# Two hybrid decoder layers on one core: five weight low halves per layer made by an adding DMA

## The chip, the cores and the metric

The kernel runs on 1 core of one Trainium2 chip. The metric is the device time of one execution in microseconds (us). Before the change three runs took 714.25, 714.69 and 716.07 us (median 714.69). The engines named here are PE (TensorE, matrix products), DVE (VectorE), ACT (ScalarE), POOL (GpSimd) and SP (SyncE, which in this kernel starts all the DMA transfers).

## The reference

Two decoder layers work on a residual stream of 256 tokens by 1024 channels, all in float32. Cut to what matters, one layer is:

```python
proj = x @ w_in                      # 1024 -> q_a, k_a, v_a, a, b, z, q_b, k_b, v_b
o_a = gdn_mixer(q_a, k_a, v_a, a, b, z, ...)   # causal conv, chunked delta rule: a 64x64
                                               # triangular system per head and chunk
o_b = moba_mixer(q_b, k_b, v_b, pos)           # partial rotary, softmax attention, 8 heads
mix = concat([o_a, o_b]) @ w_out
x = layer_norm(alpha * x + mix)
hid = causal_dwconv(x @ w_up) + b
gate, val = split(hid)
x = layer_norm(alpha * x + (silu(gate) * val) @ w_down)
```

## The kernel before, in words

All weights come as chunks of 128 partitions by 1024 float32 (512 KB). PE multiplies in a rounded form of float32 (the tile type F32R), so every weight chunk `w` is taken as a rounded high half `h` and a low half `w - h`, and the stream `x` as `xh` and `xl` in the same way. A projection (`proj`) is 24 matmuls: eight pairs `h*xh` and `h*xl`, then eight `lo*xh`. A chunk is loaded by SP into one of six `wr` buffers (`load_raw`, line 181), ACT copies its two halves of 512 columns into a `wh` tile (line 196, which rounds), and DVE (POOL for some chunks of the MLP) subtracts, `wl = wr - wh` (line 197). There are five `wh` and five `wl` buffers, so the splitting runs up to five chunks ahead of PE. A projection writes one of two PSUM buffers `pj`. ACT and DVE must empty it before the next projection but one may begin: for the delta-rule heads ACT makes a first tap (line 424) and DVE three more (line 427), for the attention heads ACT copies (line 447), DVE shuffles and multiplies (lines 449 and 450), and POOL finishes the rotary (lines 455 and 456, the unit `rp`; here called the ropes).

The mixing stage of a layer is written as a list of units, the string `ORDER[l]`: `ka:0` is the projection of head 0 of `k_a`, `qb:3` of pair 3 of `q_b`, `kk`, `decay`, `sk`, `am` build the triangular matrices A (lines 505 and 507 on DVE), `solve` inverts the 16x16 diagonal blocks on POOL (28 dependent instructions, lines 527 and 529) after a way through DRAM (`da`, line 512, `T<-da`, line 518), `ex` brings the inverses back through DRAM (`dx`, line 531, `PT<-dx`, line 538) and spreads them on DVE (line 543), `lt` is the first matmul on them (PE, line 560). Letters behind `@` keep a unit's instructions on that engine behind those of the unit before. Within these bounds a scheduler places the instructions; each engine then works through its own list in order, and an instruction that waits holds up all behind it on that engine.

Three tiles outside the split rings matter: `oh` and `ol` (the two halves of the mixer's output, needed late in a layer; `oh` also takes the raw input at the very start) and `lnb` (the rows of a layer norm, needed at a layer's two norms). In the kernel before `oh` and `ol` are taken at the top of a layer.

Of the kernel before, what the change touches and what calls it, by code (L numbers as in the profile page):

```python
# [11 lines left out]
F32 = mybir.dt.float32  # L12
F32R = mybir.dt.float32r
# [3 lines left out]
AF = mybir.ActivationFunctionType  # L17
OP = mybir.AluOpType
# [51 lines left out]


ORDER = ("""
ab ka:0@A ab2@G ka:2@P qb:0@GP ka:3@G ka:1 kk:0 decay@AGD kk:1@PG kb:0@G kb:2@G sk@GP ld:0@P ld:1@DG kb:3@G am:0@A
vb:1@DAGP qb:1@GP kb:1@G rp@DG am:1@AG qb:2@G qb:3 va:2@GP va:0@G va:3 rk@G solve@G va:1@D qa:1 qa:0@P ex@DPA lt@GP s:0@DA lx@DAP
tr:0@AD mt:32:0@GAP mx:32:0@G mt:32:1@G vt:0@G rp@GP mx:32:1@PAG pv:0 mt:64:0@GDPA mt:64:1@AG s:1@AGD
qa:3@G qa:2@GP mx:64:0@PG tr:1@PA mx:64:1@D z:0 s:2@GADP pv:1@GA sq:0@DG vt:1@ADP zsol:0@D az tr:2@A s:3@GDP pv:2@AG
tr:3@PGD zsol:1@A z:2@G qk@GP sq:1@GDA o:0@ADP z:1@G wu:1@PGA pv:3@AGP o:1@GDP w:0:5 w:0:4@D w:1:4@PDA z:3@PD w:1:6@G
w:0:7@GD w:1:5@GPD ot:1@AP ot:0@G wu:0@PA w:0:6@A
""", """
vb:1@APDG ab@GD ka:0@G ab2@G ka:3 qb:0@P ka:2@G ka:1@P kk:0 decay@ADG kb:0 kk:1@GA kb:2 sk@AP kb:3@G kb:1@PG qb:2  # L80
rp@GPD qb:3@GP am:0@PA qb:1@DP am:1@AG ld:0@GP va:1@P va:0@GP rk@AG va:2@G ld:1@D solve@GP va:3@P qa:1 ex@D lt@DAP s:0@GD
lx@DAPG mt:32:0@A mt:32:1@AG vt:0@PD rp@GAD tr:0@AP qa:0 mx:32:0 pv:0@A mx:32:1@AD mt:64:0@AGD mt:64:1@DGP s:1@A
qa:3 qa:2@P mx:64:1@APD tr:1@P z:0@G s:2@G sq:0@D vt:1@DG mx:64:0@GDP pv:1 zsol:0@DGP az@A tr:2@DA s:3@GD pv:2@AG
# [6 lines left out]
def hybrid_kernel(ctx, tc, xT, x, wab, wch, par, lnrow, cst, msk, out):  # L90
    nc = tc.nc
    pe, act, dve, pool, sp = nc.tensor, nc.scalar, nc.vector, nc.gpsimd, nc.sync
# [5 lines left out]
    res = ctx.enter_context(tc.tile_pool(name="res", bufs=1))  # L98
# [104 lines left out]
    def load_chunk(l, ci, hp=None, le=None):  # L203
        return split(load_raw(l, ci), hp, le)

    def proj(ps, l, ci, le=None):
        h, lo = load_chunk(l, ci, le=le)
        h = h.rearrange("p (k m) -> p k m", k=KT)
        lo = lo.rearrange("p (k m) -> p k m", k=KT)
        for k in range(KT):  # L210
            pe.matmul(ps, h[:, k, :], xh[:, k, :], start=k == 0, stop=False)  # L211
            pe.matmul(ps, h[:, k, :], xl[:, k, :], start=False, stop=False)  # L212
        for k in range(KT):
            pe.matmul(ps, lo[:, k, :], xh[:, k, :], start=False, stop=k == KT - 1)  # L214
# [12 lines left out]
    def rsqrt(v, n, eng):  # L227
# [3 lines left out]
        for i in range(2):  # L231
# [106 lines left out]
    vb = vb_first()  # L338
    const_prep()

    for l in range(DEPTH):
# [24 lines left out]
        qb, kb = mt("qb", [128, 4, S]), mt("kb", [128, 4, S])  # L366
# [3 lines left out]
                st[nm] = mt("vz", [128, 2, HG, 128] if nm != "va" else [128, HG, S], 2)  # L370
            return st[nm]

        oh = res.tile([128, KT, S], F32R, name="oh")
        ol = res.tile([128, KT, S], F32R, name="ol")
        G, T, st = [], {}, {}

        def u_ab():
            abr = small.tile([128, KT, 8], F32, name="abr", bufs=1)
# [277 lines left out]
        def u_pv(p):  # L656
            PT0, PT1 = st["PT", p]
            po = ps_m()[:, 0:256]
            for a in range(2):
                rs = slice(64 * a, 64 * a + 64)  # L660
                hs = slice((2 * p + a) * 64, (2 * p + a) * 64 + 64)
                pe.matmul(po[rs, :], vb[:, 0, hs], PT0[:, a, :], start=True, stop=False, skip_group_check=True)  # L662
                pe.matmul(po[rs, 128:256], vb[:, 1, hs], PT1[:, a, :], start=False, stop=True, skip_group_check=True)
            act.activation(oh[:, 4 + p, :], po, AF.Copy)
            dve.tensor_tensor(ol[:, 4 + p, :], po, oh[:, 4 + p, :].bitcast(F32), op=OP.subtract)

        def u_vt(b):
            ps = heads(ps_a())
# [46 lines left out]
        def u_ot(b):  # L715
            bs = slice(b * 128, b * 128 + 128)
            ps = heads(ps_m())
            for h in range(HG):
                pe.transpose(ps[:, h, :], st["on", b][:, h, :], ident)
            of = mt("PT0", [128, HG, 128], 2)  # L720
            dve.scalar_tensor_tensor(of, ps, pr[:, P_NG:P_NG + 1], zs[:, :, bs], op0=OP.mult, op1=OP.mult)
            act.activation(oh[:, 0:4, bs], of, AF.Copy)
            dve.tensor_tensor(ol[:, 0:4, bs], of, oh[:, 0:4, bs].bitcast(F32), op=OP.subtract)

        acc = []

# [14 lines left out]
        def w_out(t, ks, stop=False):  # L741
            ts = slice(t * 128, t * 128 + 128)
            if not acc:
                acc.extend([[ps_a() for _ in range(2)] for _ in range(2)])
            start, done[t] = not done[t], done[t] + list(ks)
            for k in ks:
                if k not in ws:
                    ws[k] = load_chunk(l, C_WO + k)
            down(t, [(oh[:, k, ts], ol[:, k, ts], ws[k]) for k in ks], start, stop)

        def u_wu(i):
            nm = ("qb", "kb", "ka", "qa")[2 * i:2 * i + 2]
# [52 lines left out]
        lnb = load_lnb(l, 0)  # L805
# [64 lines left out]
        lnb = load_lnb(l, 1)  # L870
# [133 lines left out]
```

## Time and profile before

| | |
|---|---|
| median of three runs | 714.69 us |
| the profiled execution | 714.04 us, of which 712.3 us from its first to its last instruction (the span) |
| granted TensorE clock, mean over the span | 0.984 |
| PE busy | 688.6 us (97%), 5056 matmuls |
| DVE busy | 576.9 us (81%) |
| ACT busy | 400.8 us (56%) |
| POOL busy | 197.2 us (28%) |
| DMA | 118.07 MB, mean 166 GB/s |

PE's busy time counts the ends of pipelined matmuls, so a "full" stretch can still hold short gaps; where PE stands still for long, its busy time in a stretch falls below the stretch's length. The clock is given as a share: 1.00 is 2.4 GHz, and a half is 1.2 GHz, the lower of its two levels. Layer 0's mixing stage runs from about 20 to 150 us, layer 1's from about 367 to 500 us; between them lie the MLPs.

### The profile page before, as it was taken

Reading aid. Unit: us, or ns where it says so; the run is one execution under the profiler, and the core shown is the slowest. Engines: PE = TensorE matmul, PEld = TensorE weight load, DVE = VectorE, ACT = ScalarE, POOL = GpSimd, SP = SyncE. Lnnn points to the kernel's source line nnn. Section 1 sums busy time; section 2 is a strip of 40 time slices with the busy share of each in tenths; the row PEclk is TensorE's granted clock in tenths of the full one; section 3 lists DMA queues with packets and bytes.
Section 4 is the critical chain, followed back from the end, with each engine's and each line's share of the span. In section 5 each row is a group of like instructions: output and inputs, shape, how many; then the busy total and the mean of one; then the engine's idle time right before and its main releaser. Section 6 shows DMA issues by size and latency. Waiting matters only on the chain.

```text
span 712.3 us, 13664 instructions
## 1 busy us (share of the span) xinstructions
PE 688.6 (97%) x5056; PEld 618.6 (87%) x5056; DVE 576.9 (81%) x1273; ACT 400.8 (56%) x908; POOL 197.2 (28%) x200
## 2 busy tenths in 40 slices
PE   8989999999999999999999989999999999999994
PEld 5979888787999999999888988888789999999994
DVE  5899877599788887778879987776998888887756
ACT  5644466546666665656355445556476566666531
POOL 0045700013333343332002382000153333333413
PEclk9999999999999999999999997999999999999998
DMA  8876351521766665656153437134246766666201
GB/s 313 305 244 192 78 198 40 199 89 61 276 220 194 211 222 184 202 181 205 60 201 129 144 94 222 61 103 159 66 150 234 233 213 194 214 206 202 70 1 60
DMA packets 41217, 118.07 MB, mean 166 GB/s; under 512 B 10176, under 2 KB 12992, under 8 KB 40640
## 3 DMA queue, kind: packets, MB, share of 16 engines
q1 hardware_dynamic: 41152, 117.21, 49.6%
q8 instruction: 40, 0.66, 0.3%
q14 instruction: 25, 0.20, 0.1%
HBM read 114.84 MB, written 2.36 MB: 165 GB/s over the span
## 4 chain that ended last, share of the span: by engine, by line
PE 86%; DVE 9%; ACT 1%; issue 1%; DMA 1%; SPq 0%; DVEq 0%; ACTq 0%
PE pj L211 16%; PE pj L212 15%; PE pj L214 15%; PE ac L732 8%; PE ac L733 8%; PE ac L734 8%; DVE wl L197 3%; PE pj L225 1%; PE pj L222 1%; DVE cv L427 1%; PE mx L619 1%; PE pj L223 1%; PE mx L313 1%; DMA wr<-in_wch_dram 1%; PE mx L662 1%
## 5 line engine op out<-in xcount | busy, mean ns | idle before, releaser
L196 ACT ACTIVATE wh<-wr 128x512 fp32r<-128x512 f32 x376 | 219.5, 622 | 108.2 <-PE pj L212 49.1
L211 PE MATMUL pj<-xh,wh 128*128 128x256 f32 x1024 | 258.6, 289 | 7.4 <-DVE cv L427 7.4
L212 PE MATMUL pj<-xl,wh 128*128 128x256 f32 x1024 | 257.2, 287 | 0.0
L197 DVE TENSOR_TENSOR wl<-wr,wh 128x512 fp32r<-128x512 f32 x292 | 206.7, 736 | 28.2 <-ACT wh L196 14.7
L211 PEld LDWEIGHTS pj<-xh,wh 128*128 128x128 f32 x1024 | 198.6, 194 | 11.4 <-issue 5.4
L212 PEld LDWEIGHTS pj<-xl,wh 128*128 128x128 f32 x1024 | 199.1, 194 | 1.6
L197 POOL TENSOR_TENSOR wl<-wr,wh 128x512 fp32r<-128x512 f32 x84 | 116.2, 1405 | 204.9 <-ACT wh L196 199.7
L214 PE MATMUL pj<-xh,wl 128*128 128x256 f32 x1024 | 147.6, 286 | 0.0
L214 PEld LDWEIGHTS pj<-xh,wl 128*128 128x128 f32 x1024 | 134.2, 194 | 0.4 <-issue 0.2
L733 PE MATMUL ac<-wh,fal 128*128 128x512 f32 x144 | 56.4, 392 | 0.0
L732 PE MATMUL ac<-wh,fah 128*128 128x512 f32 x144 | 56.1, 392 | 0.0
L734 PE MATMUL ac<-wl,fah 128*128 128x512 f32 x144 | 56.0, 389 | 0.0
L842 DVE TENSOR_TENSOR fal<-fth,fah 128x256 fp32r<-128x256 f32 (+1 forms) x48 | 36.8, 767 | 17.3 <-ACT fah L841 17.0
L828 DVE SCALAR_TENSOR_TENSOR fc<-pj,par,fc 128x255 f32<-128x255 f32 x80 | 38.1, 476 | 4.2 <-ACT fc L824 2.8
L828 DVE SCALAR_TENSOR_TENSOR fc<-pj,hw,fc 128x255 f32<-128x255 f32 x80 | 38.3, 478 | 3.7 <-ACT fc L824 2.4
L817 POOL TENSOR_SCALAR hw<-par 128x66 f32<-128x66 f32 x2 | 2.1, 1048 | 139.2 <-DVE wlh L197 139.2
L839 DVE SCALAR_TENSOR_TENSOR fth<-fth,fc 128x256 f32<-128x256 f32 (+1 forms) x48 | 23.6, 492 | 20.1 <-ACT fth L838 20.1
L841 ACT ACTIVATE fah<-fth 128x256 fp32r<-128x256 f32 (+1 forms) x48 | 18.9, 393 | 34.8 <-DVE fth L840 34.8
L838 ACT ACTIVATE fth<-fc 128x256 f32<-128x256 f32 (+1 forms) x48 | 19.2, 400 | 31.7 <-DVE fc L828 31.5
L427 DVE SCALAR_TENSOR_TENSOR cv<-pj,par,cv 128x255 f32<-128x255 f32 (+2 forms) x72 | 33.8, 472 | 0.6 <-ACT cv L424 0.3
L734 PEld LDWEIGHTS ac<-wl,fah 128*128 128x128 f32 x144 | 27.1, 188 | 5.9
L732 PEld LDWEIGHTS ac<-wh,fah 128*128 128x128 f32 x144 | 27.1, 189 | 4.8
(257 smaller groups left out, 1030.5 us busy)
## 6 DMA issues: line engine op xcount, KB each, us to landing
wr<-in_wch_dram SPq DMA_DIRECT2D x195, 512.0 KB, 4.1
lnb<-in_lnrow_dram SPq DMA_DIRECT2D x4, 1024.0 KB, 4.6
xres<-in_x_dram SPq DMA_DIRECT2D x2, 512.0 KB, 6.8
da<-A SPq DMA_DIRECT2D x4, 256.0 KB, 3.4
ka<-in_wch_dram SPq DMA_DIRECT2D x2, 512.0 KB, 4.5
qa<-in_wch_dram SPq DMA_DIRECT2D x2, 512.0 KB, 5.1
qb<-in_wch_dram SPq DMA_DIRECT2D x2, 512.0 KB, 4.8
kb<-in_wch_dram SPq DMA_DIRECT2D x2, 512.0 KB, 5.7
```

What stands on the lines that cost most here:

```text
L196: ih = act.activation(h[:, s], raw[:, s], AF.Copy)
L197: il = le.tensor_tensor(lo[:, s], raw[:, s], h[:, s].bitcast(F32), op=OP.subtract)
L211: pe.matmul(ps, h[:, k, :], xh[:, k, :], start=k == 0, stop=False)
L212: pe.matmul(ps, h[:, k, :], xl[:, k, :], start=False, stop=False)
L214: pe.matmul(ps, lo[:, k, :], xh[:, k, :], start=False, stop=k == KT - 1)
L427: dve.scalar_tensor_tensor(cv[:, o:], ps[:, :S - o], w[:, j:j + 1], cv[:, o:], op0=OP.mult, op1=OP.add)
L732: pe.matmul(ps, a_h, w_h[:, ns], start=start and i == 0, stop=False, skip_group_check=True)
L733: pe.matmul(ps, a_l, w_h[:, ns], start=False, stop=False, skip_group_check=True)
L734: pe.matmul(ps, a_h, w_l[:, ns], start=False, stop=stop and i == len(items) - 1, skip_group_check=True)
L828: dve.scalar_tensor_tensor(cv[:, d], ps[:, d.start - o:d.stop - o], w[:, q:q + 1], cv[:, d], op0=OP.mult, op1=OP.add)
L839: dve.scalar_tensor_tensor(th, th, 1.0, cg[:, ts], op0=OP.add, op1=OP.mult)
L842: dve.tensor_tensor(al, th, ah.bitcast(F32), op=OP.subtract)
```

## The change

For five chunks of a layer the low half is no longer made by DVE. A unit `p:n`, placed in the order ahead of the projection that uses its chunk, loads the chunk as before; ACT writes the rounded high half into one half of a tile and the same number negated into the other; a DMA that POOL starts then reads the chunk once more from DRAM and adds it onto the negated half, which leaves `w - h` there. The tile is `oh`, `lnb` or `ol`, at a time when the layer does not hold anything else in it; `oh` and `ol` are taken for the mixer's output only at its first write (`mo`). `proj` takes a prepared pair from `pre` where there is one. The chunks are `kb:0`, `kb:2`, `kb:3` in both layers, then `qb:3` and `va:2` in layer 0, `qb:1` and `va:0` in layer 1.

```diff
+PRE = (((C_KB, "oh"), (C_KB + 2, "ol"), (C_KB + 3, "lnb"), (C_QB + 3, "oh"), (C_VA + 2, "ol")),
+       ((C_KB, "oh"), (C_KB + 2, "ol"), (C_KB + 3, "lnb"), (C_QB + 1, "oh"), (C_VA, "ol")))
...
-ab ka:0@A ab2@G ka:2@P qb:0@GP ka:3@G ka:1 kk:0 decay@AGD kk:1@PG kb:0@G kb:2@G sk@GP ld:0@P ld:1@DG kb:3@G am:0@A
+ab ka:0@A p:0 ab2@G ka:2@P p:1 qb:0@GP p:2 ka:3@G ka:1 kk:0 decay@AGD kk:1@PG kb:0@G kb:2@G sk@GP ld:0@P ld:1@DG kb:3@G p:3 am:0@A
...
+    pre = {}
+
+    def sum_split(l, ci, home):
+        raw = load_raw(l, ci)
+        both = res.tile([128, 2, 1024], F32R, name=home)
+        for v, sign in ((0, 1.0), (1, -1.0)):
+            for q in range(0, 1024, 512):
+                i = act.activation(both[:, v, q:q + 512], raw[:, q:q + 512], AF.Copy, scale=sign)
+                if "act" in hold:
+                    tc.add_manual_dep(i.ins, hold["act"].name, nosync, reason="norm first")
+        pool.dma_start(both[:, 1, :], wch[l, ci], accum_op=OP.add)
+        pre[l, ci] = both[:, 0, :], both[:, 1, :]
+
     def proj(ps, l, ci, le=None):
-        h, lo = load_chunk(l, ci, le=le)
+        h, lo = pre.pop((l, ci), None) or load_chunk(l, ci, le=le)
...
-        oh = res.tile([128, KT, S], F32R, name="oh")
-        ol = res.tile([128, KT, S], F32R, name="ol")
         G, T, st = [], {}, {}
+
+        def mo(name):
+            if name not in st:
+                st[name] = res.tile([128, KT, S], F32R, name=name)
+            return st[name]
+
+        def u_p(n):
+            ci, home = PRE[l][n]
+            sum_split(l, ci, home)
```

In the changed kernel line numbers are 2 higher above the new helper (198 is the ACT copy of a split, 199 the subtraction, 215 the new ACT copies, 218 the adding DMA) and 22 higher in the units (477 and 478 are the ropes, 449 the taps).

On POOL, layer 0, from the start of the list to the rotary of `kb:2` (`km` are masks, `gx` belongs to the decay, `sw` to the rotary), there stood before:

```order
L167 CAST km<-wr 128x640
L455 ISA
L455 TENSOR_TENSOR sw<-sw,kt 128x256
L418 TENSOR_TENSOR gx<-kt,g_l 128x512 x2
L456 TENSOR_TENSOR qb<-qb,sw 128x256
L455 TENSOR_TENSOR sw<-sw,kt 128x256
L456 TENSOR_TENSOR kb<-kb,sw 128x256
```

and now:

```order
L218 DMA oh<-in_wch_dram 128x1024
L218 DMA ol<-in_wch_dram 128x1024
L218 DMA lnb<-in_wch_dram 128x1024
L169 CAST km<-wr 128x640
L440 ISA
L440 TENSOR_TENSOR gx<-kt,g_l 128x512 x2
L218 DMA oh<-in_wch_dram 128x1024
L218 DMA ol<-in_wch_dram 128x1024
L477 TENSOR_TENSOR sw<-sw,kt 128x256 x2
L478 TENSOR_TENSOR qb<-qb,sw 128x256
```

Three adding DMAs stand ahead of the masks, two more ahead of all ropes; the last of them (for `va:2`) reuses the tile of `kb:2`, so it waits until PE is through with `kb:2` and ACT has then written four copies.

On ACT, layer 0, around the decay (`E`) and the emptying of `kb:0` and `kb:2`, there stood before:

```order
L465 ACTIVATE E_243<-ac 128x4x128
L465 ACTIVATE E_244<-ac 128x512
L447 ACTIVATE kb<-pj 128x256
L196 ACTIVATE wh<-wr 128x512 x2
L471 ACTIVATE E_243<-ac 128x4x128
```

and now:

```order
L469 ACTIVATE kb<-pj 128x256
L487 ACTIVATE E_243<-ac 128x4x128
L487 ACTIVATE E_244<-ac 128x512
L215 ACTIVATE oh<-wr 128x512 x3
L493 ACTIVATE E_243<-ac 128x4x128
L215 ACTIVATE oh<-wr 128x512
L198 ACTIVATE wh<-wr 128x512 x6
L469 ACTIVATE kb<-pj 128x256
L215 ACTIVATE ol<-wr 128x512 x4
```

Eight new copies stand between the emptyings of PSUM, and six copies of later chunks come ahead of them.

On DVE, layer 0, from the decay's `gx` to the third head of `ka`, there stood before:

```order
L413 CAST g_h<-g 128x8
L197 TENSOR_TENSOR wl<-wr,wh 128x512
L414 TENSOR_TENSOR g_l<-g,g_h 128x8
L418 TENSOR_TENSOR gx<-kt,g_h 128x512 x2
L427 SCALAR_TENSOR_TENSOR cv<-pj,par_216,cv 128x254
L197 TENSOR_TENSOR wl<-wr,wh 128x512
L427 SCALAR_TENSOR_TENSOR cv<-pj,par_216,cv 128x253
L427 SCALAR_TENSOR_TENSOR cv<-pj,par_216,cv 128x255
L197 TENSOR_TENSOR wl<-wr,wh 128x512
L430 SCALAR_TENSOR_TENSOR ka<-th,cv 128x256
```

and now:

```order
L435 CAST g_h<-g 128x8
L472 TENSOR_TENSOR qb<-qb,kt 128x256
L436 TENSOR_TENSOR g_l<-g,g_h 128x8
L440 TENSOR_TENSOR gx<-kt,g_h 128x512 x2
L449 SCALAR_TENSOR_TENSOR cv<-pj,par_216,cv 128x255
L199 TENSOR_TENSOR wl<-wr,wh 128x512
L449 SCALAR_TENSOR_TENSOR cv<-pj,par_216,cv 128x254
L199 TENSOR_TENSOR wl<-wr,wh 128x512
L449 SCALAR_TENSOR_TENSOR cv<-pj,par_216,cv 128x253
L519 SCALAR_TENSOR_TENSOR scr,sk<-ac,kt 128x128
```

The subtractions that stand here now are those of `ka:1`; those of `kb:0`, which stood here before, are gone.

## Rows read from the trace of the kernel before

**Rows 1.** Stretches: length, busy PE, PEld, DVE, ACT, POOL, clock, DMA share, GB/s.

```profile
20.00:30.00 10.00, 10.00 (x84) 9.73 (x83) 9.46 (x26) 8.36 (x19) 0.72 (x1) 1.00 0.79 264
30.00:46.00 16.00, 14.16 (x98) 12.36 (x96) 16.00 (x48) 8.59 (x18) 6.09 (x5) 1.00 0.67 227
46.00:70.00 24.00, 23.97 (x196) 23.57 (x195) 23.80 (x68) 11.19 (x25) 12.06 (x11) 1.00 0.73 240
70.00:76.00 6.00, 3.95 (x20) 3.98 (x21) 4.76 (x10) 1.31 (x4) 4.98 (x14) 0.72 0.36 110
380.00:392.00 12.00, 11.19 (x82) 9.86 (x81) 11.94 (x32) 5.98 (x14) 4.67 (x4) 1.00 0.35 116
...
416.00:424.00 8.00, 5.96 (x38) 5.51 (x36) 6.11 (x14) 3.39 (x7) 6.82 (x16) 0.79 0.13 51
424.00:437.00 13.00, 11.38 (x103) 10.47 (x99) 11.78 (x21) 6.04 (x14) 7.79 (x16) 1.00 0.42 101
437.00:448.00 11.00, 11.00 (x157) 10.34 (x153) 7.55 (x24) 4.97 (x17) 0.00 (x0) 0.53 0.65 240
```

**Rows 2.** The chain of waits, 58 to 76 us: start, duration, engine and line.

```profile
66.32 1.75 DVE wl L197 x3
...
70.99 0.41 DVE cv L427
...
71.42 0.49 DVE cv L427
...
72.05 0.43 PE pj L211
```

**Rows 3.** Groups of DVE, 28 to 72 us: busy us, mean ns.

```profile
L197 DVE TENSOR_TENSOR wl<-wr,wh 128x512 fp32r<-128x512 f32 x29 | 21.2, 745 | 0.0
```

**Rows 4.** Groups of ACT, 20 to 46 us.

```profile
L196 ACT ACTIVATE wh<-wr 128x512 fp32r<-128x512 f32 x22 | 12.3, 623 | 0.0
```

**Rows 5.** The chain of waits, 46 to 60 us.

```profile
48.85 0.96 PE pj L214 x8
```

**Rows 6.** Groups of POOL, 31 to 64.3 us: the ropes ahead of the solve.

```profile
L455 POOL TENSOR_TENSOR sw<-sw,kt 128x256 f32<-128x256 f32 x6 | 5.1, 853 | 15.2 <-DVE sw L449 12.4 <-DVE pl L409 2.8
L456 POOL TENSOR_TENSOR kb<-kb,sw 128x256 f32<-128x256 f32 x4 | 3.5, 877 | 1.7 <-DVE kb L450 1.3 <-DVE rsz L236 0.4
...
L456 POOL TENSOR_TENSOR qb<-qb,sw 128x256 f32<-128x256 f32 x2 | 2.2, 1115 | 0.4 <-DVE qb L450 0.4
```

**Rows 7.** Timeline of POOL, layer 0: the solve's first and last but one step.

```profile
66.06 2.14 POOL L527 TENSOR_TENSOR T<-T,P 64x14 f32<-64x14 f32 x1 [1.88 <-DVE P L524]
...
81.16 0.27 POOL L527 TENSOR_TENSOR T<-T,P 64x14 f32<-64x14 f32 x1
```

**Rows 8.** Timeline of SP's DMA queue, layer 0: the inverses are read back.

```profile
85.32 0.38 SPq L538 DMA_DIRECT2D PT<-dx  x1
```

**Rows 9.** Timeline of DVE, 89 to 93 us: the first inverse is spread.

```profile
90.98 0.42 DVE L543 TENSOR_TENSOR gX<-PT,kt 128x256 f32<-128x256 f32 x1
```

**Rows 10.** Timeline of PE, layer 0: the first matmul on the inverses.

```profile
91.45 0.66 PE L560 MATMUL ac<-gX,A 64*64 64x32 f32 x16
```

**Rows 11.** Timeline of ACT, 396 to 398 us: the emptying of `kb:2`, layer 1.

```profile
397.09 0.37 ACT L447 ACTIVATE kb<-pj 128x256 f32<-128x256 f32 x1
```

**Rows 12.** Timeline of POOL, layer 1: the solve's first step.

```profile
412.82 0.60 POOL L527 TENSOR_TENSOR T<-T,P 64x14 f32<-64x14 f32 x1 [1.07 <-DVE P L524]
```

**Rows 13.** Timeline of SP's DMA queue, layer 1: the inverses are read back.

```profile
432.32 0.38 SPq L538 DMA_DIRECT2D PT<-dx  x1
```

**Rows 14.** Timeline of PE, layer 1: the first matmul on the inverses.

```profile
436.66 0.66 PE L560 MATMUL ac<-gX,A 64*64 64x32 f32 x16
```

**Rows 15.** DMA issues by line: count, KB each, median us to landing.

```profile
wr<-in_wch_dram SPq DMA_DIRECT2D x195, 512.0 KB, 4.1
...
kt<-in_cst_dram SPq DMA_DIRECT2D x1, 522.0 KB, 8.4
...
PT<-dx SPq DMA_DIRECT2D x2, 128.0 KB, 3.3
```

More of the change, by code (lines that the diff above doesn't have):

```diff
@@ L72 @@
 ORDER = ("""
-ab ka:0@A ab2@G ka:2@P qb:0@GP ka:3@G ka:1 kk:0 decay@AGD kk:1@PG kb:0@G kb:2@G sk@GP ld:0@P ld:1@DG kb:3@G am:0@A
-vb:1@DAGP qb:1@GP kb:1@G rp@DG am:1@AG qb:2@G qb:3 va:2@GP va:0@G va:3 rk@G solve@G va:1@D qa:1 qa:0@P ex@DPA lt@GP s:0@DA lx@DAP
+ab ka:0@A p:0 ab2@G ka:2@P p:1 qb:0@GP p:2 ka:3@G ka:1 kk:0 decay@AGD kk:1@PG kb:0@G kb:2@G sk@GP ld:0@P ld:1@DG kb:3@G p:3 am:0@A
+vb:1@DAGP p:4 qb:1@GP kb:1@G rp@DG am:1@AG qb:2@G qb:3 va:2@GP va:0@G va:3 rk@G solve@G va:1@D qa:1 qa:0@P ex@DPA lt@GP s:0@DA lx@DAP
 tr:0@AD mt:32:0@GAP mx:32:0@G mt:32:1@G vt:0@G rp@GP mx:32:1@PAG pv:0 mt:64:0@GDPA mt:64:1@AG s:1@AGD
@@ L79 @@
 """, """
-vb:1@APDG ab@GD ka:0@G ab2@G ka:3 qb:0@P ka:2@G ka:1@P kk:0 decay@ADG kb:0 kk:1@GA kb:2 sk@AP kb:3@G kb:1@PG qb:2
+vb:1@APDG ab@GD ka:0@G p:0 ab2@G ka:3 p:1 qb:0@P p:2 ka:2@G ka:1@P kk:0 decay@ADG kb:0 kk:1@GA kb:2 sk@AP kb:3@G p:3 kb:1@PG p:4 qb:2
 rp@GPD qb:3@GP am:0@PA qb:1@DP am:1@AG ld:0@GP va:1@P va:0@GP rk@AG va:2@G ld:1@D solve@GP va:3@P qa:1 ex@D lt@DAP s:0@GD
@@ L663, in u_pv @@
                 pe.matmul(po[rs, 128:256], vb[:, 1, hs], PT1[:, a, :], start=False, stop=True, skip_group_check=True)
-            act.activation(oh[:, 4 + p, :], po, AF.Copy)
-            dve.tensor_tensor(ol[:, 4 + p, :], po, oh[:, 4 + p, :].bitcast(F32), op=OP.subtract)
+            act.activation(mo("oh")[:, 4 + p, :], po, AF.Copy)
+            dve.tensor_tensor(mo("ol")[:, 4 + p, :], po, mo("oh")[:, 4 + p, :].bitcast(F32), op=OP.subtract)
         def u_vt(b):
@@ L721, in u_ot @@
             dve.scalar_tensor_tensor(of, ps, pr[:, P_NG:P_NG + 1], zs[:, :, bs], op0=OP.mult, op1=OP.mult)
-            act.activation(oh[:, 0:4, bs], of, AF.Copy)
-            dve.tensor_tensor(ol[:, 0:4, bs], of, oh[:, 0:4, bs].bitcast(F32), op=OP.subtract)
+            act.activation(mo("oh")[:, 0:4, bs], of, AF.Copy)
+            dve.tensor_tensor(mo("ol")[:, 0:4, bs], of, mo("oh")[:, 0:4, bs].bitcast(F32), op=OP.subtract)
         acc = []
@@ L748, in w_out @@
                     ws[k] = load_chunk(l, C_WO + k)
-            down(t, [(oh[:, k, ts], ol[:, k, ts], ws[k]) for k in ks], start, stop)
+            down(t, [(mo("oh")[:, k, ts], mo("ol")[:, k, ts], ws[k]) for k in ks], start, stop)
         def u_wu(i):
```

## The prediction

> **What bounds the kernel now.** I read the stretches first. Over most of the program PE is full and the clock stands at 1.00, and there nothing that DVE does less can help. The exceptions that the change can reach lie in the first half of each mixing stage [rows 1]. In layer 0 PE is busy 14.16 of the 16 us from 30 to 46 and 3.95 of the 6 us from 70 to 76, while DVE is busy for all of the former and for 23.80 of the 24 us between. In layer 1 PE lacks 0.81 us from 380 to 392, 2.04 from 416 to 424 and 1.62 from 424 to 437. The reader is to see that DVE is the full engine ahead of each gap. The chain of waits names the instruction: before PE goes on at 72.05 it runs through DVE alone, subtractions of weights (line 197) and the taps that empty PSUM (line 427) in turn [rows 2]. So PE waits for a PSUM buffer, and the buffer's taps wait in DVE's list behind subtractions. The groups give their weight: 29 subtractions, 21.2 us of the 44 us from 28 to 72, 0.745 us each [rows 3].
>
> The gaps cost a second time through the clock. It is 0.72 over 70 to 76 and 0.79 over 416 to 424, right where PE stood still, so part of these stretches ran at the lower level, 1.2 GHz: (1 - 0.72) * 6 = 1.7 us and (1 - 0.79) * 8 = 1.7 us [rows 1]. Recoverable are 1.84 + 2.05 + 1.7 = 5.6 us in layer 0 and 0.81 + 2.04 + 1.62 + 1.7 = 6.2 us in layer 1. The clock of 0.53 from 437 to 448 belongs to a stretch of small matmuls behind a gap; I leave it out of the sum.
>
> A second chain runs beside this one, on POOL: ropes, then the solve, then two transfers through DRAM, then the first matmul on the inverses (line 560). PE meets it at 91.45 and at 436.66 [rows 10, 14]. The read-back starts at 85.32 and 432.32 [rows 8, 13] and lands a median 3.3 us later [rows 15], at 88.6 and 435.6; DVE then needs 0.42 us [rows 9]. So PE arrives only 2.4 us (91.45 - 88.6 - 0.42) and 0.6 us after the inverses could be there. If PE gains more than that, the solve must move too. This is the gate of the whole change.
>
> **The change part by part.** *DVE* loses ten subtractions per layer, 10 * 0.745 = 7.5 us [rows 3]: six (`kb:0`, `kb:2`, `kb:3`) ahead of the matrices A, four behind. The gap at 70 is 2.05 us, so DVE's backlog there goes; what is late next is the gate.
>
> *ACT* gets twenty copies where it had ten, 10 * 0.56 = 5.6 us more per layer (12.3 / 22 = 0.56 back to back [rows 4]). In layer 0 twelve of the twenty come before 32 us, into a stretch where ACT is busy 8.36 of 10 already [rows 1]; six copies more are 3.4 us against the 1.64 us left. Since `ka:2` to `ka:1` are split just ahead of PE there, I count PE 1 us late (bounds 0 and 1.8). From 30 to 70 ACT is busy 19.8 of 40 us, so the other copies hide behind PE's work; without that cover they would cost at most 2.2 us, one group of four. In layer 1 the first copies fall between the norm's steps, where ACT waits; I take 0.
>
> *POOL* gets five DMA starts per layer. No row shows a DMA started by POOL. The nearest are SP's DMA instruction, 0.38 us [rows 8], and POOL's longest step of the solve, 2.14 us [rows 7]; I take 1 us. They matter by their place. The last two stand ahead of all ropes, and the last waits until PE is done with `kb:2` and ACT has written four copies (2.2 us). In layer 0 `kb:2` ended at 48.85 + 0.96 = 49.8 [rows 5]; with 1.84 us of gap gone and 1 us lost to ACT I put it at 48.5 to 49. Then 2.2 + 1 us, so the ropes begin near 52, where before they were spread from 31 on. Their twelve instructions last 5.1 + 3.5 + 2.2 = 10.8 us [rows 6]: POOL is ready for the solve at 62.5. DVE's part (line 524) was what the solve waited for before, 1.88 us [rows 7]; it follows A, which loses six subtractions (4.5 us) ahead of it, so it comes at about the same time. The solve begins near 62.5 instead of 66.06, 3.5 us earlier. In layer 1 `kb:2` was emptied at 397.09 [rows 11]; 1.1 us earlier, plus 2.2 + 1 + 10.8, gives 410.0 against 412.82 [rows 12], 2.8 us earlier.
>
> The Trainium skill (SBUF — State Buffer, section "SBUF: two separate sides") holds a rule against this: descriptors of a DMA started on GpSimd cannot be written while DVE runs in a two-port mode, and it tells of 620 ns that became 3100. No row here shows such a DMA; an estimate by that page would put each start 2.5 us later. It is taken up under the gate rival.
>
> *The adding transfer* has no row either. Below it lies a plain chunk, 4.1 us; above, twice the slowest of that size, 2 * 8.4 = 16.8 us, as it reads DRAM and the tile [rows 15]. I take twice the plain one, 8 us. It has time: PE takes 24 * 0.12 = 2.9 us per chunk (0.96 / 8 a matmul [rows 5]); between `kb:2` and `va:2` lie five chunks, and the low half is wanted 16 matmuls later, 48.7 + 14.4 + 1.9 = 65, against a start at 51. That is 14 us free; in layer 1, with six chunks, 17. The engines' share is 0.73 at most stretches here [rows 1], so ten more transfers fit; plain loads run several chunks ahead.
>
> **The sum.** Layer 0: PE could be at line 560 at 91.45 - 5.6 + 1 = 86.9; the gate opens at 88.6 - 3.5 + 0.42 = 85.5. PE decides: 4.6 us gained. Layer 1: PE could be there at 430.5; the gate opens at 435.6 - 2.8 + 0.42 = 433.2. The gate decides: 3.4 us, and PE waits 2.7 us. Gaps of 2 us have brought 1.7 us of lower clock at 70 and 416, so I take off one such stretch. 4.6 + 3.4 - 1.7 = 6.3 us. The profiled execution took 714.04 us (span 712.3 and 1.7 around it), 0.65 under the median; so 707.7 for it, 708.4 for the median. What follows line 560 is full on PE, so the gain stays.
>
> **The rivals.** *The gate does not move.* POOL starts its ropes late, or a start lasts 4 to 5 us, and the solve begins when it did. Then the gains are 2.4 and 0.6 us, less 1.7 for the clock: 1.3 us, 713.4. For it: POOL's list puts two waiting starts ahead of twelve ropes. Against: POOL waited 1.88 and 1.07 us for DVE before [rows 7, 12]. The page's estimate above would give this time as well.
>
> *The solve shortens too.* The same step takes 2.14 us at 66.06, amid subtractions, and 0.27 at 81.16 [rows 7]. With DVE ahead of its work the first steps may lose 3 us; PE then decides in both layers, 4.6 + 6.2 us, and no new gap lowers the clock: 10.8 us, 703.9; if the stretch of 0.53 goes as well, 702. For that the Trainium skill (SBUF — State Buffer, section "Who interferes with whom") has a rule: a DVE instruction with two SBUF inputs contends with GpSimd's reads. By that rule the time is this rival's; the trace agrees, with 2.14 against 0.27.
>
> *The adding transfer is slow,* which ends on the other side. Past 14 us, PE stands at `va:2` in layer 0, us for us; past 17 at `va:0` in layer 1. At 22 us: layer 0 4.6 - 8 = -3.4, layer 1 gets 3.4 - (5 - 2.7) = 1.1, and long gaps lower the clock in both, -3.4: 5.7 us slower, 720.4. It decides from about 18 us. For it: the transfer reads two sources and shares the engines with loads that took 8.4 us in a crowd. Against: the median of 4.1.
>
> That the change doesn't do what it says I give nothing: the lists of both kernels show the subtractions gone.
>
> **How the numbers follow.** The forecast has 0.58, with its own range 704.5 to 711.5 (ACT's loss 0 to 1.8, the lower clock 0 to 3.4). The gate rival has 0.17, the shorter solve 0.10, the slow transfer 0.15. A difference under 0.3%, 2.1 us, is about what a measurement of this kernel cannot tell from none. So faster is 0.58 + 0.10 = 0.68, the same 0.17, slower 0.15. The range goes from 702.5, nearly all of the shorter solve, to 717, which takes in the gate rival and the nearer half of the slow transfer. The predicted time is 708.5.
>
> **What would show it.** DVE at line 449 without a wait of PE on it near 70 and 416, and fewer than 23 us busy of 24 from 46 to 70: the first step is right. The solve's first step at 62 to 63.5 and 409 to 411: the gate moved; at 66 or later, the gate rival. PE's line 582 (560 before) near 87 and 433. A wait of PE at `va:2` or `va:0` on the DMA into `ol`: the slow transfer. I am wrong if ACT's copies at line 215 hold the emptying of PSUM back by more than 2 us, or if POOL's starts last longer than 4 us.

## The result, and the profile after

The changed kernel takes 724.78 us (median of four runs, 723.15 to 728.11) against 715.38 us for the kernel before on the same chip: the ratio is 1.0134, with a 95% interval from 1.0103 to 1.0165. It is 1.3% slower, where 708.5 us was forecast, and it lies outside the stated range (702.5 to 717). The profiled execution took 726.39 us, with a span of 724.6 us. Executions that came out over 1.5% above the fastest of their kernel, at a lower granted clock, are left out of the medians and ratios below.

The stretches of the changed kernel come first, with the columns of [rows 1] (busy PE, PEld, DVE, ACT, POOL, then clock, DMA share, GB/s).

```profile
20.00:30.00 10.00, 9.78 (x79) 9.25 (x77) 7.83 (x26) 9.87 (x23) 1.90 (x2) 1.00 0.79 216
30.00:46.00 16.00, 12.74 (x95) 11.43 (x94) 13.14 (x37) 7.21 (x17) 4.44 (x4) 1.00 1.03 343
46.00:70.00 24.00, 24.00 (x194) 23.61 (x193) 21.16 (x58) 14.72 (x32) 11.29 (x14) 1.00 0.89 258
70.00:76.00 6.00, 1.55 (x13) 1.34 (x12) 4.37 (x10) 1.15 (x2) 3.14 (x3) 1.00 0.36 113
```

DVE has room now: 13.14 us busy of 16 and 21.16 of 24, where it was full before [rows 1]. What is full instead is the last but one column: the DMA share went from 0.67 to 1.03 between 30 and 46, from 0.73 to 0.89 between 46 and 70. And from 70 to 76, where PE was busy 3.95 us, it is busy 1.55. Layer 1 runs 11 us later than before, so its stretches don't stand line against line. The one in which its first three adding transfers land and the one behind its inverses are these:

```profile
376.00:391.00 15.00, 11.83 (x86) 10.71 (x85) 8.40 (x20) 7.60 (x17) 0.86 (x1) 0.97 0.98 310
...
452.00:463.00 11.00, 10.81 (x215) 9.62 (x215) 9.76 (x27) 7.76 (x26) 0.00 (x0) 1.00 0.36 115
```

and the same work as the first of them before the change, 11 us earlier:

```profile
365.00:380.00 15.00, 15.00 (x114) 13.91 (x113) 12.34 (x36) 9.32 (x21) 0.00 (x0) 1.00 0.70 234
```

The DMA share is 0.98 there too (0.70 before), and PE loses 3.2 us of 15 where it was full before; but the small matmuls behind the inverses run at 1.00, where the clock was 0.53 [rows 1]. What PE lost is one wait. ACT stood 5.2 us for a plain chunk, the subtraction and the taps came late behind it, and PE stood 3.2 us for the taps (start, duration, instruction, and in brackets the idle time before it and what ended it):

```profile
386.47 1.15 ACT L198 ACTIVATE wh<-wr 128x512 fp32r<-128x512 f32 x2 [5.17 <-DMA wr<-in_wch_dram]
```

```profile
389.70 0.36 PE L226 MATMUL pj<-xh,wh 128*128 128x256 f32 x1 [3.17 <-DVE sd L425]
```

The DMA queues and some of the DMA issues of the changed kernel (packets, MB, share of 16 engines; then count, KB each, median us to landing):

```profile
q1 hardware_dynamic: 41152, 117.21, 48.6%
q0 software_dynamic: 1440, 5.24, 4.0%
...
oh<-in_wch_dram POOLq DMA_DIRECT2D x4, 512.0 KB, 7.2
ol<-in_wch_dram POOLq DMA_DIRECT2D x4, 512.0 KB, 9.1
...
lnb<-in_wch_dram POOLq DMA_DIRECT2D x2, 512.0 KB, 9.4
da<-A SPq DMA_DIRECT2D x4, 256.0 KB, 6.8
```

and of the kernel before:

```profile
q1 hardware_dynamic: 41152, 117.21, 49.6%
...
da<-A SPq DMA_DIRECT2D x4, 256.0 KB, 3.4
```

The queue q0 carries only the ten adding transfers. Their engine time is 0.040 * 724.6 * 16 / 10 = 46.4 us each; a plain chunk of the same size cost 25.3 us before (49.6% of 16 * 712.3 us, shared out over 117.21 MB). And A's way to DRAM (`da`) takes a median of 6.8 us where it took 3.4. The plain chunks are hit as well where the transfers crowd. Of those that SP asked for from 20 to 40 us, this is the time to landing before the change:

```profile
DMA to landing us min/median/max: 3.3/4.0/8.0
```

and now:

```profile
DMA to landing us min/median/max: 5.0/12.2/13.4
```

How PE comes to stand still near 71 is read from four timelines: DVE, PE (its last row is of layer 1), POOL, and SP's DMA queue.

```profile
55.59 4.80 DVE L472 TENSOR_TENSOR kb<-kb,kt 128x256 f32<-128x256 f32 x1
...
71.60 0.57 DVE L545 TENSOR_TENSOR P<-T,km 64x256 f32<-64x256 f32 x1 [2.69 <-DMA T<-da]
...
88.47 3.49 DVE L199 TENSOR_TENSOR wl<-wr,wh 128x512 fp32r<-128x512 f32 x1
```

```profile
78.41 0.55 PE L226 MATMUL pj<-xh,wh 128*128 128x256 f32 x1 [6.86 <-DVE cv L449]
...
93.02 0.36 PE L226 MATMUL pj<-xh,wh 128*128 128x256 f32 x1 [2.30 <-DVE cv L449]
...
102.37 0.66 PE L582 MATMUL ac<-gX,A 64*64 64x32 f32 x16
...
452.33 0.66 PE L582 MATMUL ac<-gX,A 64*64 64x32 f32 x16
```

```profile
54.34 0.86 POOL L218 DMA_DIRECT2D ol<-in_wch_dram  x1 [4.57 <-ACT ol L215]
...
72.71 1.20 POOL L549 TENSOR_TENSOR T<-T,P 64x14 f32<-64x14 f32 x1 [4.88 <-DVE P L546]
```

```profile
54.30 0.33 SPq L307 DMA_DIRECT2D lnb<-in_lnrow_dram  x1
61.08 0.94 SPq L534 DMA_DIRECT2D da<-A  x2
...
67.38 0.68 SPq L540 DMA_DIRECT2D T<-da  x1
```

Before the change SP's queue had:

```profile
54.54 1.37 SPq L512 DMA_DIRECT2D da<-A  x2
...
58.74 0.69 SPq L518 DMA_DIRECT2D T<-da  x1
```

Read from the end: PE waits 6.9 us for the taps that empty its PSUM buffer (line 449). The taps stand in DVE's list behind the solve's first step on DVE (line 545), which waits for the blocks of A to come back (`T<-da`) until 71.6; they could be asked for only at 67.4, once A had landed, and A was sent at 61.1, 6.5 us later than before. Before, the same read-back let the solve begin at 66.06 [rows 7], now at 72.71. A second wait of PE, 2.3 us ahead of 93.02, is for taps behind a subtraction that lasted 3.49 us beside POOL's next run of ropes (0.73 us is the mean of line 199). The first matmul on the inverses comes at 102.37 instead of 91.45 [rows 10]: 10.9 of the 12.3 us that the span grew. In layer 1 it is at 452.33 against 436.66 [rows 14]. That is 15.7 us later, 4.8 more than in layer 0; of these, 3.4 us come back behind it, where the clock is better.

### The profile page after: what moved, and what is told of

Same layout as the page of the kernel before. It is cut to its first block, busy times and chain, and to the rows that moved or that the text cites. A ratio compares the mean times of both kernels' runs of the same rounds, so it can differ in the third digit from the quotient of the medians.

```text
span 724.6 us, 13659 instructions
## 1 busy us (share of the span) xinstructions
PE 688.3 (95%) x5056; PEld 618.0 (85%) x5056; DVE 572.3 (79%) x1253; ACT 410.2 (57%) x928; POOL 198.4 (27%) x210
## 3 DMA queue, kind: packets, MB, share of 16 engines
q1 hardware_dynamic: 41152, 117.21, 48.6%
## 5 line engine op out<-in xcount | busy, mean ns | idle before, releaser
L198 ACT ACTIVATE wh<-wr 128x512 fp32r<-128x512 f32 x356 | 208.3, 622 | 92.6 <-PE pj L227 46.5
L226 PE MATMUL pj<-xh,wh 128*128 128x256 f32 x944 | 239.7, 290 | 16.1 <-DVE cv L449 12.9
L227 PE MATMUL pj<-xl,wh 128*128 128x256 f32 x944 | 237.8, 288 | 0.0
L199 DVE TENSOR_TENSOR wl<-wr,wh 128x512 fp32r<-128x512 f32 x272 | 191.6, 733 | 35.3 <-ACT wh L198 24.4
L226 PEld LDWEIGHTS pj<-xh,wh 128*128 128x128 f32 x944 | 184.2, 195 | 19.9 <-issue 14.3
L227 PEld LDWEIGHTS pj<-xl,wh 128*128 128x128 f32 x944 | 184.7, 196 | 1.6
L229 PE MATMUL pj<-xh,wl 128*128 128x256 f32 x944 | 136.1, 286 | 1.3 <-DVE wl L199 1.3
L229 PEld LDWEIGHTS pj<-xh,wl 128*128 128x128 f32 x944 | 123.5, 194 | 2.2 <-DVE wl L199 1.7
```

The source lines that it names most:

```text
L198: ih = act.activation(h[:, s], raw[:, s], AF.Copy)
L199: il = le.tensor_tensor(lo[:, s], raw[:, s], h[:, s].bitcast(F32), op=OP.subtract)
```

## The experiments

All times are medians, all ratios are to the kernel before on the same chip. Two theories stood at the start. **Burst**: POOL's rotary products, queued behind the start of `p:4`, run in one stretch and hold DVE (the 4.80 us above), so A is late. **Crowd**: the adding transfers fill the DMA engines, so A's transfers and the loads are late.

**Three early units only, two late units only.** Left out are `p:3 p:4`, then `p:0 p:1 p:2`.

> Only p:0 to p:2 of each layer; qb:3 and va:2 (layer 0), qb:1 and va:0 (layer 1) are split by DVE again, so no DMA start stands ahead of the ropes on POOL. Theory 'burst': in the changed kernel the ropes, held behind the start of p:4, run in one stretch; one DVE product of the rotary (line 472) lasts 4.8 us instead of 0.4 to 1.0 beside it, the matrix A and with it SP's list come late, and PE stands 7.0 us at 71. Then no product at line 472 lasts over 1.2 us, the gaps at 71 and 90 are gone, while those at 36 and 43 (3.6 us) stay: 714 to 717 us. Theory 'crowd': the adding transfers slow the plain loads down (12 us instead of 4 to 6 from 27 to 34 us), and this is what makes PE wait everywhere; with three of five transfers left at the same places the early gaps stay and about half of the later loss: 718 to 721 us.

718.42 us, 1.0059 (1.0032 to 1.0086).

> Only p:3 and p:4 of each layer. Burst: the ropes still stand behind p:4's start, DVE is still held over 4 us once per layer, PE still stands 5 to 7 us near 70: 719 to 723 us, and no gap over 1.7 us before 60. Crowd: the early transfers are gone and the plain loads before 45 us take 4 to 6 us again; the later loss halves: 716 to 719 us.

714.52 us, 0.9992 (0.9970 to 1.0015). The losses don't add up to 1.0134: three units cost 0.6%, two nothing, five 1.3%. The DMA share was 1.04 from 30 to 46 with the early three, and 0.68 there with the late two. The late two came out under both theories' numbers. In their profile line 582 begins at 94.23 in layer 0, 2.8 us later than before the change, and the span is 713.1 against 712.3 us: layer 0 loses, and layer 1 gives most of it back.

**The ropes freed from `p:4`'s start.**

```diff
-kb:1@G rp@DG am:1@AG
+kb:1@G rp@D am:1@AG
...
-rp@GPD qb:3@GP
+rp@PD qb:3@GP
```

> All five units, but the letter G is taken from the unit rp of both layers, so that the ropes need not stand behind p:4's start on POOL: they are spread among the two starts. Every transfer and every ACT copy stays. Burst: no product at line 472 over 1.5 us, the solve starts near 63 to 66, the gap at 71 is under 2 us: 713 to 717 us. Crowd: nothing changes that matters, 721 to 725 us.

724.34 us, 1.0138 (1.0113 to 1.0163): no gain. The lists of DVE and SP are those of the changed kernel, only POOL's differs (and a few rows of PE and ACT). DVE's timeline of this kernel:

```profile
53.41 0.97 DVE L472 TENSOR_TENSOR kb<-kb,kt 128x256 f32<-128x256 f32 x1
56.34 0.82 DVE L472 TENSOR_TENSOR kb<-kb,kt 128x256 f32<-128x256 f32 x1
...
71.70 0.57 DVE L545 TENSOR_TENSOR P<-T,km 64x256 f32<-64x256 f32 x1 [6.02 <-DMA T<-da]
```

and its SP queue:

```profile
57.84 1.07 SPq L534 DMA_DIRECT2D da<-A  x2
...
66.97 0.68 SPq L540 DMA_DIRECT2D T<-da  x1
```

DVE is held no more, A is sent at 57.84 instead of 61.08, and yet line 545 begins at 71.70, as late as in the changed kernel: A lay 3 us longer among the transfers. The burst theory falls here. What sets the time of the solve in these two kernels is how fast the engines clear what is queued on them.

**The adding transfers cut to 8 columns.**

```diff
-        pool.dma_start(both[:, 1, :], wch[l, ci], accum_op=OP.add)
+        pool.dma_start(both[:, 1, 0:8], wch[l, ci][:, 0:8], accum_op=OP.add)
```

> The changed kernel with every adding transfer cut to 8 of 1024 columns: the rest of the addition is left out, its ACT copies, POOL starts and the order of every engine stay. Burst: DVE is still held over 4 us behind p:4's start and PE still stands 4 to 7 us at 71; only the gaps at 36 and 43 go: 718 to 721 us. Crowd: plain loads take 4 to 6 us again, the gaps go with it: 707 to 712 us.

717.94 us, 1.0035 (1.0006 to 1.0064). The expectation was wrong in one point: the scheduler placed the work anew when the transfer was short, so the lists are not those of the changed kernel, and the run separates less than it was meant to. A loss stays without the traffic. With the ropes freed as well:

> The adding transfers cut to 8 of 1024 columns and the ropes freed as well: of the change there remain ACT's ten more copies per layer, POOL's five starts and the places of the loads. If the ropes' late run is what is left of the loss: 711 to 714 us. If ACT's copies and the loads' places are: 716 to 719 us, like the tiny transfers alone.

722.55 us, 1.0107 (1.0052 to 1.0161); neither of the two expectations. All lists but POOL's and a few rows of PE are those of the run before it. PE stood 3.28 us near 91 in both profiles, but from 90 to 150 us the clock was 0.86 here and 0.97 there (the shortest of that run's ten executions). Why it stayed low for longer is open.

**No subtraction at all, and nothing in its place.**

```diff
+        if ci in SKIP[l]:
+            raw = load_raw(l, ci)
+            h = lo = whp.tile([128, 1024], F32R, name="wh")
...
```

> The kernel before, in which the five chunks of a layer that the change takes have no low half of their own (the rounded high half stands for it): ten subtractions per layer are left out, and there is no other copy, no DMA start of POOL and no transfer in their place. This is the most that taking them from DVE can bring. Theory 'DVE's subtractions are the bound' (that of the prediction, 6.3 us and 1 us of ACT): 706 to 709 us. Theory 'the gaps pass on' (PE then meets the wait for the inverses, and DVE is held by POOL's ropes behind the solve): 711 to 714 us.

708.47 us, 0.9909 (0.9872 to 0.9945): DVE's relief is worth as much as the prediction said, but it does not come in the way that it said. POOL's timeline, two stretches, and PE's first matmuls on the inverses (line 570 here) in the profile, which is of the longest of five executions (711.16 us):

```profile
62.87 1.88 POOL L537 TENSOR_TENSOR T<-T,P 64x14 f32<-64x14 f32 x1 [0.92 <-DVE P L534]
```

```profile
70.00:76.00 6.00, 5.92 (x48) 5.84 (x48) 5.54 (x12) 3.09 (x8) 4.98 (x14) 1.00 0.02 4
...
437.00:448.00 11.00, 10.90 (x234) 9.66 (x232) 9.47 (x27) 8.34 (x26) 0.00 (x0) 1.00 0.63 224
```

```profile
91.61 0.60 PE L570 MATMUL ac<-gX,A 64*64 64x32 f32 x14
...
436.09 0.48 PE L570 MATMUL ac<-gX,A 64*64 64x32 f32 x10
```

The gap at 70 is gone, with the clock at 1.00 there against 0.72 [rows 1], and the solve begins at 62.87. (That it is near the forecast 62.5 is chance: the forecast was for ropes held behind the start of `p:4`, which this kernel does not have.) But PE reaches the inverses at 91.61 and 436.09, where it was at 91.45 and 436.66 before [rows 10, 14]: no earlier in layer 0, 0.6 us earlier in layer 1. The gain lies behind them. From 437 to 448 the clock is 1.00 against 0.53 [rows 1], which is (1 - 0.53) * 11 = 5.2 us.

**Copying instead of adding.**

```diff
-        pool.dma_start(both[:, 1, :], wch[l, ci], accum_op=OP.add)
+        pool.dma_start(both[:, 1, :], wch[l, ci])
```

> The changed kernel, with the five DMAs of POOL copying the chunk over the tile and not adding to it (the low half is then the chunk itself); order, starts, bytes read from DRAM and bytes written to the tile stay. If the bytes alone crowd the engines: about 46 us of engine time for each of these transfers as before, 722 to 726 us. If it is the adding: about 25 us of engine time each, as for a plain chunk, the gap at 71 shrinks to some 3 us: 717 to 720 us.

716.39 us, 1.0018 (0.9997 to 1.0039). Every list is that of the changed kernel, row by row, so the 1.16% between the two ratios (8.3 us) are the adding alone. Its queue, one stretch, and DVE at the solve's first step:

```profile
q0 software_dynamic: 1440, 5.24, 2.2%
```

```profile
30.00:46.00 16.00, 14.36 (x104) 12.97 (x103) 14.33 (x41) 9.03 (x20) 4.13 (x4) 1.00 0.90 338
```

```profile
67.66 0.59 DVE L545 TENSOR_TENSOR P<-T,km 64x256 f32<-64x256 f32 x1 [0.82 <-DMA T<-da]
```

0.022 * 715.6 * 16 / 10 = 25.2 us of engine time per transfer, as much as a plain load; adding costs 46.4 / 25.2 = 1.84 times that for the same bytes from DRAM. A's blocks are back 4 us earlier, 2 of them because A was sent at 59.03. That is not all that the adding costs: with copying, line 582 begins at 99.28 and 443.39, 3.1 and 8.9 us earlier than with adding. In layer 1 the wait of 3.2 us for a plain chunk is absent, and the clock is 1.00 from 380 to 392 and from 416 to 450, where it was 0.93 from 380 to 392 and 0.91 from 424 to 437 with adding.

Is the held DVE a loss that the crowd only hid? The copy with the ropes freed says no:

> The fourth of a square: adding or copying, ropes behind p:4's start or freed from it. With adding, freeing the ropes changed nothing (724.8 and 724.3 us); copying behind the start took 716.4 us, and there a product of the rotary on DVE lasted 4.5 us beside POOL's run of ropes and the matrix A was sent at 59.0 us. The low half is again the chunk itself. If the run of ropes that holds DVE is a loss that the crowd only hid: no product over 2 us, A sent at 55 to 56.5 us, 711 to 714 us. If it costs nothing even without the crowd: 715.5 to 718 us, and what is left over the 708.5 us without subtractions lies in the loads' places and the copies.

718.36 us, 1.0043 (1.0015 to 1.0071). No product on line 472 lasts over 0.96 us there, yet A is sent at 58.2, not at 55 to 56.5, and its blocks are not back earlier. With the late two alone DVE was not held even with the ropes behind the start (0.99 us at most), so this last run could tell little:

> p:3 and p:4 alone, with the ropes freed from standing behind p:4's start. The two late transfers alone did not crowd the engines for long (714.5 us). If the held DVE (a product of 1 to 5 us beside the ropes) costs anything there: 711 to 713 us. If not: 714 to 715.5 us.

716.06 us, 1.0014 (0.9987 to 1.0041).

**What is left between copying (716.4) and no subtraction (708.5).** First without any DMA of POOL, then with ACT's copies at the old count:

```diff
-        pool.dma_start(both[:, 1, :], wch[l, ci], accum_op=OP.add)
...
-        for v, sign in ((0, 1.0), (1, -1.0)):
+        for v, sign in ((0, 1.0),):
```

> The changed kernel without any DMA of POOL: the negated half is used as it stands for the low half (the addition is left out). Of the change there remain the units' loads at their new places, twenty copies of ACT per layer and DVE's ten subtractions fewer. With the transfers cut to 8 columns the same kernel took 717.9 us, without any of the change's work on ACT and POOL 708.5. If POOL's starts (and the ropes and waits behind them) make up these 9 us: 708 to 711 us. If ACT's copies or the loads' places do: 715 to 718 us.

714.92 us, 1.0000 (0.9973 to 1.0027).

> As the copies alone, but ACT writes only the rounded half (ten copies per layer, as many as before the change), which also stands for the low half: there remain only the new places of the units' loads and copies, and the ten subtractions fewer. If ACT's ten further copies cost: 708 to 710 us here, 3 us or more under the copies alone. If the places cost: within 1.5 us of the copies alone.

718.12 us, 1.0024 (0.9991 to 1.0057). The run without ACT's further copies is not the faster one, so they are not the loss, and the starts with the bytes copied are at most a small part of it. Then both with the units put back, right ahead of the projections that use them:

```diff
-ab ka:0@A p:0 ab2@G ka:2@P p:1 qb:0@GP p:2 ka:3@G ka:1
+ab ka:0@A ab2@G ka:2@P qb:0@GP ka:3@G ka:1
...
-kk:1@PG kb:0@G kb:2@G sk@GP ld:0@P ld:1@DG kb:3@G p:3 am:0@A
+kk:1@PG p:0 kb:0@G p:1 kb:2@G sk@GP ld:0@P ld:1@DG p:2 kb:3@G am:0@A
```

> The kernel with the places alone (ten subtractions and the five low halves left out, no copy more than before, no DMA of POOL: 718.1 us), but each unit p:n now stands right ahead of the projection that uses its chunk, as the loads did before. If the early places cost: 707 to 710 us, like the 708.5 us without subtractions. If not: within 2 us of 718.

709.45 us, 0.9929 (0.9901 to 0.9956).

> The same, with ACT writing the negated half as well (ten copies per layer more; it stands for the low half). If ACT's copies are hidden beside PE's work: within 1.5 us of the places put back alone. If ACT is late with them: 3 us or more above it.

707.37 us, 0.9912 (0.9878 to 0.9946). The early places cost 0.9% in both pairs, and ACT's ten further copies cost nothing that these intervals (0.3% either way) can tell. The solve's first step, POOL, with the copies early:

```profile
68.28 4.78 POOL L548 TENSOR_TENSOR T<-T,P 64x14 f32<-64x14 f32 x1 [4.94 <-DVE P L545]
```

and with the copies put back:

```profile
64.40 2.74 POOL L548 TENSOR_TENSOR T<-T,P 64x14 f32<-64x14 f32 x1 [4.13 <-DVE P L545]
```

One link in it could be that SP sends the norm's rows (`lnb`, 1 MB) right ahead of A when `kb:3` sits in that tile. Without `p:2`:

> The copies alone at the early places (714.9 us), without the unit p:2 of each layer, so that kb:3 is split by DVE as before and the tile lnb stays free: SP sends the rows of the norm (1 MB) four chunks ahead of the matrix A again, not between. The negated half still stands for the low half of the other four chunks. If the early places cost because that load goes out next to A's transfers: A lands within 3 us of its sending, the solve starts near 64, 708 to 711 us. If they cost for another reason: 714 to 717 us.

714.02 us, 1.0001 (0.9976 to 1.0026). The norm's rows then go out four chunks before A, whose transfers took 2.4 and 2.6 us, and the solve begins at 66.40 instead of 68.28, and yet the time stayed (`kb:3`'s two subtractions are back on DVE in it, a fifth of the relief): that link is not most of the loss. With the copies early A is sent at 57.4, without `p:2` at 57.0, put back at 54.0. What in the early places delays it was not found.

The two profiles show where much of the price falls. The stretch of small matmuls behind the inverses, with the copies early:

```profile
90.00:106.00 16.00, 14.06 (x174) 13.19 (x175) 10.53 (x30) 7.85 (x24) 0.00 (x0) 0.60 0.64 208
```

and with the copies put back:

```profile
90.00:106.00 16.00, 14.77 (x292) 12.06 (x291) 11.36 (x33) 8.86 (x29) 0.00 (x0) 0.94 0.54 202
```

The clock is 0.60 against 0.94, which is 5.4 of the 9.3 us by which their spans differ (715.1 and 705.8); PE had stood 3.27 us just ahead of it in the one and 2.47 in the other. The median clocks of all their executions, 0.991 and 0.993, are nearer to each other (1.4 us), so these profiles do not show how much of the 0.9% is the clock.

**Adding, with the units put back; the same in layer 1 alone.**

> The changed kernel whole (it computes the reference), with each unit p:n right ahead of the projection that uses its chunk, as with the places put back. If the places and the adding are two separate losses (7.4 and 8.4 us): 716 to 718 us, the places' part won back. If the later start puts the adding transfers (7 to 10 us from start to landing) on PE's path: 722 us or more.

722.01 us, 1.0082 (1.0050 to 1.0114): with the adding on, the places win back 0.5% (3.7 us), not 0.9%, so the two losses don't simply add up. The time is that of the second expectation, but not its mechanism: PE waits for no transfer in the trace.

> The same in layer 1 alone; layer 0 as before the change. Layer 1's stretch had DMA shares of 0.35 to 0.7 before. If the adding costs only where the engines are short of room: 711 to 713 us. If it costs in layer 1 too: 714 to 717 us.

714.36 us, 0.9984 (0.9958 to 1.0010): layer 1's five units together gain nothing that this can tell. By the expectation that is the case in which the adding costs in layer 1 too, about as much as the relief of DVE brings there (that share is argued, no run has it alone). The 1.0% between these two runs is what layer 0's five units lose.

**A few adding transfers where there is room.** The late two in layer 1 alone, then with `va:2` in layer 0:

> Only p:3 and p:4, and only in layer 1, where the engines' DMA share around them was 0.3 to 0.7 before. If two adding transfers with room around them let DVE's four subtractions fewer through: 711.5 to 713 us, less than the kernel before. If their waits eat the gain: 714 to 715.5 us.

711.37 us, 0.9955 (0.9932 to 0.9977).

> p:3 and p:4 in layer 1 (alone they took 711.4 us) and p:4, the low half of va:2, in layer 0. If one adding transfer at 51 us finds room there: 710 to 711.5 us. If it delays the matrix A's way through DRAM as the five did: 713 to 715 us.

709.12 us, 0.9910 (0.9885 to 0.9936): 0.9% faster than the kernel before, and so faster than both. Its stretches:

```profile
30.00:46.00 16.00, 13.51 (x95) 11.74 (x94) 15.55 (x45) 10.07 (x21) 6.17 (x6) 1.00 0.75 237
46.00:70.00 24.00, 23.75 (x191) 23.13 (x190) 23.69 (x67) 10.07 (x22) 12.43 (x11) 1.00 0.80 260
70.00:76.00 6.00, 4.78 (x39) 4.31 (x39) 5.35 (x12) 3.67 (x8) 4.90 (x15) 1.00 0.28 91
...
437.00:448.00 11.00, 10.91 (x232) 9.70 (x233) 9.47 (x28) 8.32 (x26) 0.00 (x0) 1.00 0.55 199
```

The DMA share stays at 0.80 in layer 0 (it is 0.91 from 380 to 392), A is sent at 55.47 and its blocks are asked for at 59.66, within 1 us of the times before, and the clock is 1.00 in the stretches that had 0.72 and 0.53 [rows 1]. The gain is in the clock: the median over its executions is 0.994 against 0.986, about 6 of the 6.4 us, and line 582 begins at 91.82 and 436.21, as line 560 did before [rows 10, 14].

## Why the prediction was wrong

Taken one behind the other, four kernels part the loss, in shares of the 714.7 us: the copies at late places -0.88% (6.3 us gained), the early places +0.88% (6.3 lost), POOL's starts and the copied bytes +0.18% (1.3, within the intervals of 0.2 to 0.4% that each ratio has), the adding +1.16% (8.3). The sum, 1.34%, is that of the changed kernel by construction. The order matters: with the adding on, the places were worth 0.5%.

- **The relief of DVE (6.3 us gained): right in size, by luck.** Leaving the subtractions out brought 6.1 us. But the sum had PE at the inverses 4.6 us earlier in layer 0 and 3.4 in layer 1, and without the subtractions it was 0.2 us later and 0.6 earlier. PE's waits did not become fewer, they moved (in layer 0 PE stood 2.5 us at 82.3, for taps behind a subtraction that lasted 3.8 us beside POOL's products). What became less is the lower clock: the runs' span times (1 - mean clock) is 3.5 us without the subtractions and 8.6 us before, and most of it is the stretch of 0.53 behind layer 1's inverses, which I had left out of the sum.
- **ACT's copies: not refuted.** Ten more per layer cost nothing that the intervals can tell; the 1 us that I took off is inside them.
- **POOL's starts (1 us): right.** They last 0.86 to 1.04 us, beside a DVE that is busy most of the time. The late starts of 2.5 us that I weighed by the Trainium skill (SBUF — State Buffer, "SBUF: two separate sides") are not in these rows.
- **The adding transfer (8 us to landing): right**, at medians of 7.2 to 9.4 us. PE never waited for one.
- **"The engines' share is 0.73 at most stretches here [rows 1], so ten more transfers fit; plain loads run several chunks ahead": this step failed.** I priced a transfer by how long it takes to land, and not by the engine time that it takes from the others. From 20 to 70 us the engines were busy 0.79 * 10 + 0.67 * 16 + 0.73 * 24 = 36.1 of 50 us [rows 1]. Five adding transfers take 5 * 46.4 / 16 = 14.5 us more: 50.6 of 50. Even five plain ones, 5 * 25.3 / 16 = 7.9 us by numbers of the profile before, would have left only 6 us free. The queue was the bound, and its victim was not the adding transfer. In layer 0 it was A's way through DRAM, which I had as the gate's chain and whose price I kept at its old value; and it was the plain chunks, 12.2 us to landing against 4.0 from 20 to 40 us, one of which ACT and then PE stood for in layer 1. The adding cost 8.3 us.
- **The gate: the right chain, the wrong link.** I let the solve start at 62.5 once POOL was through with the ropes. POOL was ready only at 67.8 (its ropes began at 54.9, not near 52, and took 12.9 us with their waits, not 10.8) and then stood 4.9 us for DVE's step, whose data came late. And DVE, waiting at that step, held up the taps: a wait that I had at line 582 of PE struck 30 us earlier, at PSUM.
- **The early places: a term that I left out, and the second step that failed.** I counted 1 us for ACT there; the places cost 6.3 us with the adding left out. The cause of that is open.
- **The rivals.** The slow transfer had the right side, and its time (720.4) is the nearest by chance: its mechanism, PE standing at `va:2`, did not happen. Of the gate rival, the late ropes happened and the start of 4 to 5 us did not; the solve then came 6.7 us later than before, not when it did. The shorter solve did not happen: from its first step to its last it took 15.2 us, 15.7 before. The stretch of 0.53, which that rival names in half a sentence, is where the relief of DVE lay.
- **The signs.** DVE's busy time from 46 to 70 fell under 23 us, as it should (21.16), but PE still waited for line 449, and for longer.

The Trainium skill has a rule that I did not weigh: Collectives: The Full Stack, "The bandwidth ceiling: the fold count and why AG ≠ RS ≠ AR" says that the add of a reduce-scatter needs two source reads, and gives 1.93 as the measured ratio of the bandwidth of an all-gather, which copies, to its own. It tells this of a ring over several cores; the 1.84 of this kernel's adding against copying is near it.

## What to carry to other kernels

A transfer has two prices: the time until it lands, which its user pays if it is near, and the engine time, which everyone else in the queue pays. Before moving work onto the DMA engines, add up their share over the stretch with the new engine time, and look for the small transfer on a chain (here A to DRAM and back) that will queue behind it; two and three such transfers in the whole program gained 0.5% and 0.9%, five in each layer lost 1.3%. An instruction that waits for such a transfer in the list of the engine that empties PSUM stops PE, here 30 us before PE's own use of the result. And where short waits of PE are followed by a stretch at the lower clock, count that stretch too: here it made up most of what DVE's relief was worth.

## What the runs showed of the hardware that was not expected

- Adding in a DMA costs 46.4 us of engine time per 512 KB, copying the same 25.2. From 20 to 40 us, with three adding transfers in the way, a plain chunk of 512 KB took a median of 12.2 us to land, 4.0 in the kernel before.
- A DVE product of two SBUF tiles lasted 4.80 us beside POOL's run of products, 0.97 where POOL's products are spread; in this kernel that was no loss, because another wait covered it. The subtraction of 3.49 us beside POOL's next run was not covered: PE stood 2.30 us behind it.
- The same kernel's runs differ with the clock that they get: the kernel before ran from 710.8 us (mean clock 0.991) to 718.3 us (0.982) in one comparison. A difference under 0.3% needs many runs here, and a cause under 2 us can't be read from two profiles.
